# Probabilities times values in three f32r products, and the two mixing norms' weights moved into w_out's rows

## The chip, the core and the metric

The kernel runs on one core of one Trainium2 chip. The metric is the device time of one execution in microseconds. The profile's engines are PE (matmul) with its weight loads shown apart as PEld, DVE (vector), ACT (scalar), POOL, and SP, which issues most DMAs. The operand type f32 is full float32. f32r ("fp32r" in the profile) is a float32 that its producer has rounded to fewer mantissa bits; the matmul rows of the profile write f32 for both.

## What is computed

One inference step of a hybrid decoder layer, for a prompt of 1024 tokens and for 8 running sequences of 8 new tokens each. Around the mixing stage stand two SwiGLU layers (width 2816) with norms. The mixing stage is what the change touches:

```python
  h = pre_mix(x); z = h @ w_in + b_in
    group A: sliding-window GQA (window 128) with learned sinks, banded blocks of 128 queries
    group B: HGRN2 gated linear recurrence, 4 heads of 128
  x = x + post_mix(concat(norm(attn_out), gate(hgrn_out)) @ w_out)

p = sink_probs(s, mask, sink)                       # softmax with a sink in the denominator
out = einsum('bnhgqk,bnkhd->bnqhgd', p, vv)         # probabilities times values
a = rms_norm(a, attn_out_norm[l])                   # over all 512 attention channels
o = rms_norm(o, hg_out_norm[l]) * silu(hg)          # over 128 channels of each head
mix = concatenate([a, o], axis=-1) @ w_out[l]
```

Each attention head has width 64; 8 query heads share 2 key/value heads (g = 0, 1). A query block of 128 sees two key blocks, its own and the one before it (the very first only its own).

## The kernel before

**Tokens.** They go in three groups: n = 0 (256 prompt tokens and the 64 sample tokens, 320 wide), n = 1 and n = 2 (384 prompt tokens each). The engines' order is made by a scheduler that places the instructions by its own simulated times; buffers come from pools with a fixed number of slots, and an instruction that fills a slot waits until the slot's last reader is done.

**Large products.** Every large matrix product is split into three (`mm3`, lines 295 to 299): each operand is a rounded part ("hi", f32r, a cast on ACT, line 274) and a remainder ("lo", DVE, line 275), and PE adds hi by hi (L297), hi by lo (L298) and lo by hi (L299). Weights are loaded by SP into `raw` (3 slots), split by `load_w` into two tiles of the pool `wsp` (8 slots, so four hi/lo pairs), and used.

**Mixing.** `w_in_units(n)` makes z; `w_out_units(n)` (lines 1466 to 1493) multiplies the normed outputs by w_out. For n = 0 it loads w_out in 8 tiles of 128 output columns, each [128, 8, 128]; for n = 1 and 2 in 8 tiles each of [128, 2, 512]. Between them, spread over the large products by `tick()`, run the generators of the attention blocks (`attn_block`, 8 of them) and of the recurrence blocks (`hgrn_block`, 8), and two more for the sample tokens.

**One attention block** goes in two halves (`pr`). Each half makes four score tiles (L1129), the masked maxima (L1137), the exponentials (L1146), then for g = 0 and 1 transposes the probabilities into one PSUM bank (L1155) and copies the bank to a tile `t` of the pool `t2` (L1158: by DVE for g = 0, by ACT for g = 1). After a `yield` the values product follows (L1168): for each head and key block one f32 matmul with the transposed probabilities [128 keys, 128 queries] as weights and the values `vn` [128 keys, 64 channels] as the moving operand. In the program these are 120 matmuls; the profile shows 240 records, two for each f32 matmul.

**Around it.** `finish_attn` scales the block's rows by the root of the mean square and by `aon`, the attention norm's weights broadcast to all partitions (L1103). The gate `z["g"]` is multiplied by the column of `hg_out_norm` (L1089). `vn` is copied out of PSUM by ACT (L1056), one tile for a group. `kv_out` and `sample_attn` store rows of `vn`. The recurrence's tiles come from the pool `m2` (6 slots), `t2` has 8 slots; `t2` also serves the norms and `xt`, the residual rows that SP loads (L441).

## Time and profile before

| what | value |
|---|---|
| median of 3 runs | 1993.19 us (1992.47 to 1993.76) |
| the profiled execution, its own time | 1995.67 us |
| its span in the profile | 1994.0 us |
| granted PE clock, mean | 0.997 |
| busy: PE, DVE, ACT, POOL | 1978.9, 1360.6, 945.8, 591.2 us |
| values product L1168 on PE | 240 records, 29.3 us |

How to read it: a row of a group gives line, engine, operation, the tile written and the tiles read, the sizes, the count, then busy time, mean length of one in ns, idle time before it and what ended that. PE records overlap, since matmuls are pipelined, so what one costs is read in the timeline from one start to the next. In the timeline a row is start, length, engine, line, operation, tiles, size, count; equal neighbours are merged. A row by windows gives for each stretch the busy time of the five engines with their counts, the clock, the DMA share and the rate.

### The profile page before, as it was taken

The numbers are of one execution on the slowest core, as the hardware profiler recorded it, in microseconds if no ns is written. First come the engines' busy times: TensorE is split into PE (matmuls) and PEld (weight loads), VectorE is DVE, ScalarE is ACT, GpSimd is POOL, SyncE is SP. The second block draws the span as 40 slices with busy tenths as digits, with TensorE's granted clock in tenths as the row PEclk, the third lists the DMA queues.
The fourth block names the chain that finished last, engine by engine and source line by source line (L and its number), as shares of the span: only waits on it lengthen the run. The fifth ranks groups of instructions, "written<-read, shape, count | busy, mean of one in ns | idle before, by whom it ended". The sixth has DMA issues, their size and how long they took to land.

```text
span 1994.0 us, 34474 instructions
## 1 busy us (share of the span) xinstructions
PE 1978.9 (99%) x13345; PEld 1856.2 (93%) x13345; DVE 1360.6 (68%) x1979; ACT 945.8 (47%) x1677; POOL 591.2 (30%) x559
## 2 busy tenths in 40 slices
PE   9999999999999999999999999999999999999998
PEld 8999999999998988798899898999999999999887
DVE  5676657886557666875566665755888888655666
ACT  7534333444455445643444555655544444444453
POOL 0013333555104002311123423301165565510202
PEclk9999999999999999999999999999999999999999
DMA  8444435555767645665444343556565555577874
GB/s 260 144 154 160 154 130 188 179 201 204 240 217 227 184 130 175 221 194 146 135 109 147 96 123 93 175 153 205 157 198 203 192 191 189 209 232 234 287 261 141
DMA packets 373694, 360.86 MB, mean 181 GB/s; under 512 B 41662, under 2 KB 295433, under 8 KB 373513
## 3 DMA queue, kind: packets, MB, share of 16 engines
q1 hardware_dynamic: 372729, 357.21, 56.9%
q8 instruction: 105, 1.72, 0.4%
q10 hardware_dynamic: 800, 1.44, 0.2%
q14 instruction: 60, 0.49, 0.1%
HBM read 280.64 MB, written 78.94 MB: 180 GB/s over the span
## 4 chain that ended last, share of the span: by engine, by line
PE 94%; DMA 2%; DVE 2%; issue 1%; ACT 0%; POOL 0%; SPq 0%; DVEq 0%; POOLq 0%; ACTq 0%
PE mm L297 28%; PE mm L299 28%; PE mm L298 28%; PE c L299 1%; PE c L297 1%; PE c L298 1%; PE pv L1168 1%; DMA raw<-in_ffn_w_gu_dram 1%; PE sc L1129 1%; PE lv L1204 1%; PE pT L1155 1%; DMA ar<-fa 1%; PE tr L518 1%; PE l L1228 0%; PE av L1283 0%
## 5 line engine op out<-in xcount | busy, mean ns | idle before, releaser
L297 PE MATMUL mm<-h,wsph 128*128 128x320 f32 (+1 forms) x1296 | 415.2, 322 | 0.0
L298 PE MATMUL mm<-h,wsph 128*128 128x320 f32 (+1 forms) x1296 | 411.0, 318 | 0.1
L299 PE MATMUL mm<-h,wspl 128*128 128x320 f32 (+1 forms) x1296 | 410.5, 317 | 0.1
L274 ACT CAST wsph<-raw 128x1024 fp32r<-128x1024 f32 x202 | 211.2, 1047 | 303.3 <-PE mm L298 235.0
L275 DVE TENSOR_TENSOR wspl<-raw,wsph 128x1024 fp32r<-128x1024 f32 x202 | 251.7, 1248 | 150.9 <-ACT wsph L274 145.6
L275 DVE TENSOR_TENSOR w<-raw,w 128x512 fp32r<-128x512 f32 (+1 forms) x226 | 245.4, 1089 | 93.9 <-ACT w L274 91.9
L274 ACT CAST w<-raw 128x512 fp32r<-128x512 f32 (+1 forms) x226 | 169.5, 754 | 213.4 <-PE mm L298 116.4
L297 PEld LDWEIGHTS mm<-h,wsph 128*128 128x128 f32 x1296 | 243.9, 189 | 5.2 <-issue 3.0
L298 PEld LDWEIGHTS mm<-h,wsph 128*128 128x128 f32 x1296 | 244.4, 189 | 2.6 <-issue 1.4
L299 PEld LDWEIGHTS mm<-h,wspl 128*128 128x128 f32 x1296 | 244.3, 189 | 1.7 <-issue 0.9
L297 PE MATMUL mm<-h,w 128*128 128x384 f32 x704 | 235.6, 335 | 0.6 <-DVE big L745 0.6
L298 PE MATMUL mm<-h,w 128*128 128x384 f32 x704 | 235.6, 335 | 0.0
L299 PE MATMUL mm<-h,w 128*128 128x384 f32 x704 | 230.3, 335 | 0.0
L297 PE MATMUL mm<-w,h 128*128 128x512 f32 x462 | 181.6, 396 | 2.3 <-DVE big L925 1.5
L729 POOL TENSOR_TENSOR big<-big 128x384 f32<-128x384 f32 x88 | 111.5, 1267 | 238.9 <-ACT big L742 127.8
L298 PE MATMUL mm<-w,h 128*128 128x512 f32 x462 | 180.5, 391 | 0.0
L299 PE MATMUL mm<-w,h 128*128 128x512 f32 x462 | 179.7, 393 | 0.0
L275 DVE TENSOR_TENSOR w<-t,w 128x512 fp32r<-128x512 f32 x176 | 158.7, 911 | 14.8 <-ACT w L274 14.6
L268 POOL TENSOR_TENSOR sm<-sm,mhalf 128x3 f32<-128x3 f32 (+4 forms) x38 | 35.7, 939 | 395.0 <-DVE sm L351 169.8
L297 PEld LDWEIGHTS mm<-h,w 128*128 128x128 f32 x704 | 132.1, 188 | 1.0 <-DVE big L745 0.9
L298 PEld LDWEIGHTS mm<-h,w 128*128 128x128 f32 x704 | 132.1, 188 | 0.0
L299 PEld LDWEIGHTS mm<-h,w 128*128 128x128 f32 x704 | 131.7, 188 | 0.1
(351 smaller groups left out, 4038.0 us busy)
## 6 DMA issues: line engine op xcount, KB each, us to landing
raw<-in_ffn_w_gu_dram SPq DMA_DIRECT2D x156, 512.0 KB
raw<-in_ffn_w_down_dram SPq DMA_DIRECT2D x74, 512.0 KB
raw<-in_w_in_dram SPq DMA_DIRECT2D x54, 512.0 KB
ar<-fa SPq DMA_DIRECT2D x70, 384.0 KB
big<-in_ffn_w_down_dram SPq DMA_DIRECT2D x88, 256.0 KB
fb<-big SPq DMA_DIRECT2D x44, 512.0 KB
raw<-fb SPq DMA_DIRECT2D x40, 512.0 KB
fa<-big SPq DMA_DIRECT2D x22, 768.0 KB
```

The source lines that it names most:

```text
L268: G.tensor_tensor(y, x, mhalf[:y.shape[0], :y.shape[1]], op=ALU.pow)
L274: S.copy(hi, src)
L275: (lo_eng or V).tensor_tensor(lo, src, hi.bitcast(F32), op=ALU.subtract)
L297: PE.matmul(out, a[0], b[0], start=first, stop=False, skip_group_check=resume)
L298: PE.matmul(out, a[0], b[1], start=False, stop=False, skip_group_check=resume)
L299: PE.matmul(out, a[1], b[0], start=False, stop=last, skip_group_check=resume)
L518: PE.transpose(bank[:, i * P:(i + 1) * P], y[kh][:, i, k * P:(k + 1) * P], ident)
L729: G.tensor_tensor(e[:, i], e[:, i], e[:, i + 1], op=ALU.mult)
L1129: PE.matmul(banks[g][:, i * 256:i * 256 + wk], zq[64 * g:64 * g + 64, 2 * pr + i, b * P:(b + 1) * P], kx[64 * g:64 * g + 64, k0:k0 + wk], ...
L1155: PE.transpose(bank[:, (i * nk + kb) * P:(i * nk + kb + 1) * P], pt[g][:, i, kb * P:(kb + 1) * P], ident)
L1168: PE.matmul(ob[:, c:c + 64], pT[g][:, (i * nk + kb) * P:(i * nk + kb + 1) * P], vn[:, vb, g * 64:g * 64 + 64], start=kb == 0, stop=kb == n ...
L1204: PE.matmul(b4[cs, a, :32], x[:, a, cs], y[:, a, cs], start=True, stop=True)
```

## The change

1. **Values product.** The transposed probabilities are split like a weight: an ACT cast and a DVE remainder for g = 0 and for g = 1, each in a tile of `t2` (four tiles a half where there were two). `vn` becomes two f32r tiles, hi and lo. The product is `mm3`, so 360 f32r matmuls of [128, 128] by [128, 64] stand where 120 f32 ones stood.
2. **Norm weights.** `attn_out_norm` and `hg_out_norm` come as eight columns in `cols`, one for each 128 rows of w_out, and `load_w` has an argument `gain`: each 128-row piece of w_out is scaled while it is split, by an ACT activation with a scale and a DVE scalar_tensor_tensor for each piece. `aon` with its two DMAs and the gate's multiplication L1089 go; L1103 becomes a tensor_scalar with the root alone.
3. **Room.** `m2` has 5 slots instead of 6, and the transposed keys `kn` go back into `K`. `vn` has 4 slots of the same size instead of 2. Where whole values are stored, `whole` adds hi and lo on DVE into a new `t2` tile first.

```diff
-    def load_w(src, pool, tag, bufs, shape=(P, KC, P)):
+    def load_w(src, pool, tag, bufs, shape=(P, KC, P), gain=None):
...
-        split(hi, lo, raw)
+        if gain is None:
+            split(hi, lo, raw)
+        for k in range(shape[1] if gain is not None else 0):
+            g = gain[:, k:k + 1]
+            S.activation(hi[:, k], raw[:, k], AF.Copy, scale=g)
+            V.scalar_tensor_tensor(lo[:, k], raw[:, k], g, hi[:, k].bitcast(F32), op0=ALU.mult, op1=ALU.subtract)
...
-            return tp.tile(list(shape), F32, tag="m2", bufs=6, name=uid("m2"))
-
-        aon = tp.tile([P, 512], F32, tag="aon", name="aon")
...
+            return tp.tile(list(shape), F32, tag="m2", bufs=5, name=uid("m2"))
...
-            vn = VN[n] = tp.tile([P, 4, P], F32, tag="vn", bufs=2, name=uid("vn"))
+            vn = VN[n] = [tp.tile([P, 4, P], F32R, tag="vn", bufs=4, name=uid("vn")) for _ in range(2)]
...
-                G.tensor_copy(vn[:, 0], VN[n - 1][:, NPB[n - 1]])
+                for new, old in zip(vn, VN[n - 1]):
+                    G.tensor_copy(new[:, 0], old[:, NPB[n - 1]].bitcast(F32))
...
-                S.copy(vn[:r, 1 + i], bank[:r, i * P:(i + 1) * P])
+                split(vn[0][:r, 1 + i], vn[1][:r, 1 + i], bank[:r, i * P:(i + 1) * P])
...
-            V.tensor_scalar(z["g"][:, :, :w], z["g"][:, :, :w], cols[:, C_HGN:C_HGN + 1], None, op0=ALU.mult)
...
-            V.scalar_tensor_tensor(o[:r], o[:r], sm[:r, 1, 0:1], aon[:r], op0=ALU.mult, op1=ALU.mult)
+            V.tensor_scalar(o[:r], o[:r], sm[:r, 1, 0:1], None, op0=ALU.mult)
...
-                    t = t2()
-                    (S.copy if g else V.tensor_copy)(t[:, :2 * wk], bank[:, :2 * wk])
-                    pT.append(t)
+                    hi, lo = [tmp2("pT", dt=F32R) for _ in range(2)]
+                    split(hi[:, :2 * wk], lo[:, :2 * wk], bank[:, :2 * wk])
+                    pT.append((hi, lo))
...
-                            PE.matmul(ob[:, c:c + 64], pT[g][:, (i * nk + kb) * P:(i * nk + kb + 1) * P],
-                                      vn[:, vb, g * 64:g * 64 + 64], start=kb == 0, stop=kb == nk - 1)
+                            cs = slice((i * nk + kb) * P, (i * nk + kb + 1) * P)
+                            mm3(ob[:, c:c + 64], [t[:, cs] for t in pT[g]],
+                                [t[:, vb, g * 64:g * 64 + 64] for t in vn], kb == 0, kb == nk - 1)
...
-            kn = m2((P, 4, P))
+            kn = K
...
+        def whole(vn, r):
+            t = tmp2("vs", (P, P))
+            V.tensor_tensor(t[:r], vn[0][:r, 3].bitcast(F32), vn[1][:r, 3].bitcast(F32), op=ALU.add)
+            return t[:r]
...
-                    wt = load_w(w_out_rows(0, 4, d * P, d * P + P) + w_out_rows(4, 8, d * P, d * P + P), pp, "wsp", 8)
+                    wt = load_w(w_out_rows(0, 4, d * P, d * P + P) + w_out_rows(4, 8, d * P, d * P + P), pp, "wsp", 8,
+                                gain=cols[:, C_AON:C_AON + 8])
...
-                    wt = load_w(w_out_rows(2 * kk, 2 * kk + 2, hf * 512, hf * 512 + 512), pp, "wsp", 8, (P, 2, 512))
+                    wt = load_w(w_out_rows(2 * kk, 2 * kk + 2, hf * 512, hf * 512 + 512), pp, "wsp", 8, (P, 2, 512),
+                                cols[:, C_AON + 2 * kk:C_AON + 2 * kk + 2])
```

The change adds 9 lines ahead of most of the places above, so the old L297 to L299 are L306 to L308 now, and the old L275 is L279.

**PE, the first half of the first attention block** (`mm` is a z tile of `w_in`, `pv` the values product's bank, `t` the transposed probabilities). Before:

```order
L299 MATMUL mm_6831<-h_6072,wspl_6828 128x320
L1168 MATMUL pv_6857<-vn_6386,t_932_6786 128x64
L1168 MATMUL pv_6857<-vn_6386,t_934_6791 128x64
L1168 MATMUL pv_6857<-vn_6386,t_932_6786 128x64
L1168 MATMUL pv_6857<-vn_6386,t_934_6791 128x64
L297 MATMUL mm_6868<-h_6071,wsph_6864 128x320
```

The same place now (the first two product groups of four; `vn_6385` and `pT_6789` are rounded parts, `vn_6386` and `pT_6790` remainders):

```order
L308 MATMUL mm_6838<-h_6074,wspl_6835 128x320
L306 MATMUL pv_6864<-vn_6385,pT_6789 128x64
L307 MATMUL pv_6864<-vn_6386,pT_6789 128x64
L308 MATMUL pv_6864<-vn_6385,pT_6790 128x64
L306 MATMUL pv_6864<-vn_6385,pT_6796 128x64
L307 MATMUL pv_6864<-vn_6386,pT_6796 128x64
L308 MATMUL pv_6864<-vn_6385,pT_6797 128x64
```

Four rows have become twelve, at the same place between the same two large products.

**DVE, while w_out's tiles for n = 0 are split** (`wspl` is a remainder, `cm`, `m` and `lv` belong to the recurrence, `big` in L1089 is the gate). Before:

```order
L275 TENSOR_TENSOR wspl_9959<-raw_9954,wsph_9958 128x1024
L1089 TENSOR_SCALAR big_9525<-big_9525,cols 128x1536
L1223 COPY_PREDICATED cm_9654<-lm_90,lv_9803 128x128
L1239 TENSOR_TENSOR m_1410_9647<-m_1410_9647,m_1412_9649 128x128x2
L275 TENSOR_TENSOR wspl_10017<-raw_10012,wsph_10016 128x1024
L1158 COPY t_1439_9849<-pT_9844 128x512
```

Now:

```order
L293 SCALAR_TENSOR_TENSOR wspl_10092<-raw_10087,cols,wsph_10091 128x128 x8
L1227 COPY_PREDICATED cm_9726<-lm_90,lv_9888 128x128
L1243 TENSOR_TENSOR m_1419_9719<-m_1419_9719,m_1421_9721 128x128x2
L293 SCALAR_TENSOR_TENSOR wspl_10164<-raw_10159,cols,wsph_10163 128x128 x8
L279 TENSOR_TENSOR pT_9949<-pT_9943,pT_9948 128x512
L279 TENSOR_TENSOR pT_9958<-pT_9952,pT_9957 128x512
```

Each remainder is eight instructions, the gate's row is gone, and one copy of a probabilities bank has become two remainders.

**SP, the end of the ffn1 pairs that run beside the first attention blocks** (`raw<-fb` are ffn weights for PE, `xt` residual rows in `t2` slots, `x1N` rows stored). Before:

```order
L900 DMA raw_8169<-fb_117 128x2x512
L441 DMA xt_7995<-in_x_prompt_dram 128x512
L441 DMA xt_7999<-in_x_prompt_dram 128x512
L441 DMA xt_8035<-in_x_prompt_dram 128x512
L441 DMA xt_8039<-in_x_prompt_dram 128x512
L441 DMA xt_8043<-in_x_prompt_dram 128x512
L441 DMA xt_8047<-in_x_prompt_dram 128x512
L444 DMA x1N_98<-big_5726 128x512
L900 DMA raw_8221<-fb_117 128x2x512
```

Now:

```order
L909 DMA raw_8286<-fb_117 128x2x512
L450 DMA xt_8044<-in_x_prompt_dram 128x512
L450 DMA xt_8048<-in_x_prompt_dram 128x512
L450 DMA xt_8100<-in_x_prompt_dram 128x512
L450 DMA xt_8104<-in_x_prompt_dram 128x512
L453 DMA x1N_98<-big_5728 128x512
L450 DMA xt_8108<-in_x_prompt_dram 128x512
L453 DMA x1N_98<-big_6008 128x512
L450 DMA xt_8112<-in_x_prompt_dram 128x512
L453 DMA x1N_98<-big_5728 128x512
L909 DMA raw_8358<-fb_117 128x2x512
```

The last two `xt` loads stand behind stores of the rows that the first ones served, and the next weight load (`raw_8221` before, counted from the loads around it `raw_8286` now) stands ahead of all six.

More of the change, by code (lines that the diff above doesn't have):

```diff
@@ L192, in gains @@
         put(C_LB, A["hg_lb_logits"].rearrange("l (c p) -> (l c) p", p=P), 8)
-        put(C_HGN, A["hg_out_norm"], 1)
+        for half in range(2):
+            nc.sync.dma_start(
+                rows[C_AON:C_AON + 4, half * 64:half * 64 + 64],
+                A["attn_out_norm"][0:1, half * 256:half * 256 + 256].rearrange("o (m d) -> (o m) d", d=64))
+        nc.sync.dma_start(rows[C_AON + 4:C_AON + 8, :], A["hg_out_norm"].partition_broadcast(4))
         bank = axbank()
@@ L321, in new_h, with tmp2 @@
         return [[hslot(n), hslot(n)], [hslot(n), hslot(n)]]
-    def tmp2(name, shape=(P, 512)):
-        return pp.tile(list(shape), F32, tag="t2", bufs=8, name=uid(name))
+    def tmp2(name, shape=(P, 512), dt=F32):
+        return pp.tile(list(shape), dt, tag="t2", bufs=8, name=uid(name))
     def bcast_steps(part, w, out):
@@ L1308, in sample_attn @@
             vsc = dr.tile([NS, P], F32, name="vsc")
-            nc.sync.dma_start(vsc, vn[:NS, 3])
+            nc.sync.dma_start(vsc, whole(vn, NS))
             vnew = tmp2("vnew", (P, 512))
@@ L1386, in sample_hgrn @@
                 PE.transpose(tb[:r, a], K[:, a, :r], ident)
-            kn = m2((P, 4, P))
+            kn = K
             V.tensor_copy(kn[:r], tb[:r])
@@ L1426, in kv_out @@
             if n == 0:
-                for i, src in ((5, kn[:r, :P]), (6, vn[:r, 3])):
+                for i, src in ((5, kn[:r, :P]), (6, whole(vn, r))):
                     for b in range(8):
```

10 lines of the change are left out of this document (3 added, 7 removed).

## Prediction

> **What bounds the kernel now.** I read the page's busy times first, then the chain that ended last, then PE's waits.
>
> ```profile
> span 1994.0 us, 34474 instructions
> PE 1978.9 (99%) x13345; PEld 1856.2 (93%) x13345; DVE 1360.6 (68%) x1979; ACT 945.8 (47%) x1677; POOL 591.2 (30%) x559
> PE 94%; DMA 2%; DVE 2%; issue 1%; ACT 0%; POOL 0%; SPq 0%; DVEq 0%; POOLq 0%; ACTq 0%
> ```
>
> PE is busy for 99% of the span and is 94% of the chain, so nearly all that is added to PE's own queue is added to the time, and what is added elsewhere costs only where it makes PE wait. The view of PE's waits has nine rows; the first and the last:
>
> ```profile
> PE mm L297 <- DVE big L925: 1.5, 1, 1.5
> ...
> PE ax L173 <- DMA rows<-in_norm_ffn_pre_dram: 0.2, 1, 0.2
> ```
>
> They sum to 7.3 us, and no wait is over 1.5 us. Faster helpers can win back a part of these 7.3 us and no more. The profiled execution took 1995.67 us, 1.67 more than its span, and 2.48 more than the median of 1993.19; I work out changes on the span and add them to the median.
>
> **The price of one small matmul.** The change turns 120 f32 matmuls into 360 f32r ones. I read what one costs in PE's timeline, from start to start, at a block that stands between large products:
>
> ```profile
> 1096.35 0.33 PE L298 MATMUL mm<-h,wsph 128*128 128x384 f32 x1
> 1096.53 0.33 PE L299 MATMUL mm<-h,wspl 128*128 128x384 f32 x1
> 1096.70 1.89 PE L1168 MATMUL pv<-vn,t 128*128 128x64 f32 x16
> 1098.40 0.48 PE L297 MATMUL mm<-wsph,h 128*128 128x512 f32 x1
> 1098.72 0.40 PE L298 MATMUL mm<-wspl,h 128*128 128x512 f32 x1
> 1098.95 0.40 PE L299 MATMUL mm<-wsph,h 128*128 128x512 f32 x1
> ```
>
> A large f32r product of 384 columns starts 0.17 to 0.18 us after the one before, one of 512 columns 0.23. The sixteen records run from 1096.70 to 1098.40, and the first product behind them lasts 0.32 us to the next start instead of 0.23, which is theirs as well: 1.70 + 0.09 = 1.79 us, 112 ns a record. The group has 240 records:
>
> ```profile
> L1168 PE MATMUL pv<-vn,t 128*128 128x64 f32 x240 | 29.3, 272 | 0.0
> L1168 PEld LDWEIGHTS pv<-vn,t 128*128 128x128 f32 x240 | 28.9, 191 | 0.3
> ```
>
> That is 240 x 0.112 = 26.9 us on PE now. What are the 112 ns made of? Other short f32 matmuls with 128-column weights tell:
>
> ```profile
> 1084.99 0.71 PE L348 MATMUL st<-omean,ss 128*128 128x1 f32 x6
> 1085.63 0.44 PE L297 MATMUL mm<-h,wsph 128*128 128x384 f32 x1
> ...
> 1157.83 0.94 PE L1290 MATMUL u<-big,m 128*128 128x128 f32 x7
> 1158.62 1.90 PE L1168 MATMUL pv<-vn,t 128*128 128x64 f32 x16
> ```
>
> With 128 moving columns a record costs 0.79 / 7 = 113 ns, with one column 0.64 / 6 = 107 ns at least, though two of these six load only 64 columns. So the price does not depend on the moving columns: it is that of getting 128 columns of weights in. The same load stands before every f32r matmul:
>
> ```profile
> L297 PEld LDWEIGHTS mm<-h,wsph 128*128 128x128 f32 x1296 | 243.9, 189 | 5.2 <-issue 3.0 <-ACT wsph L274 0.3
> 707.11 0.19 PEld L299 LDWEIGHTS mm<-wsph,h 128*128 128x128 f32 x1
> 707.33 0.13 PEld L297 LDWEIGHTS mm<-wsph,h 128*64 128x64 f32 x1
> ```
>
> An f32r load of 128 columns is recorded with 189 ns against 191 for the f32 one, and half the columns take 0.06 us less, so it too pays by the column. In the large products it hides, because 320 to 512 moving columns last longer; with 64 columns nothing hides it. I therefore price an f32r product of 64 columns at 112 ns: 360 x 0.112 = 40.3 us, **13.4 us more than now, all on PE**. The bounds: from above, the one-column row with its whole tail (0.64 us and the 0.11 by which the next start comes late, over six) gives 124 ns, so 44.6 us, +17.7. From below, the bare 1.70 / 16 = 106 ns for the new ones gives 38.2, +11.3. Far below lies the bare streaming of 64 columns: (0.230 - 0.175) / 128 = 0.43 ns a column from the 512- and 384-column paces above, so 0.175 - 320 x 0.00043 = 37 ns; that is a rival, not my value, because no short matmul above comes near it.
>
> **DVE and ACT, the probabilities.** In each of 16 halves one DVE copy and one ACT copy become two casts and two remainders. The nearest rows are the copies and the split of the block's output, which also reads PSUM:
>
> ```profile
> L1158 DVE COPY t<-pT 128x512 f32<-128x512 f32 x14 | 9.5, 682 | 1.9 <-PE pT L1155 1.7
> L1158 ACT COPY t<-pT 128x512 f32<-128x512 f32 x14 | 8.2, 588 | 13.4 <-PE pT L1155 13.4
> L1095 DVE TENSOR_TENSOR h<-oT,h 128x512 fp32r<-128x512 f32 x8 | 5.4, 680 | 0.0
> ```
>
> DVE gets 16 x 0.68 = 10.9 us more, ACT 16 x 0.59 = 9.4 us, and the way from transposes to values product grows from one copy, 0.68 us, to two casts and a remainder, 2 x 0.59 + 0.68 = 1.86 us: 1.2 us longer. The cover is the time between copy and product:
>
> ```profile
> 1133.77 0.68 DVE L1158 COPY t<-pT 128x512 f32<-128x512 f32 x1
> 1133.86 0.59 ACT L1158 COPY t<-pT 128x512 f32<-128x512 f32 x1 [4.98 <-PE pT L1155]
> ...
> 1137.42 1.89 PE L1168 MATMUL pv<-vn,t 128*128 128x64 f32 x16
> ...
> 1310.35 0.59 ACT L1158 COPY t<-pT 128x512 f32<-128x512 f32 x1 [2.48 <-PE pT L1155]
> ...
> 1312.51 0.33 PE L1168 MATMUL pv<-vn,t 128*128 128x64 f32 x2
> ```
>
> 3.0 us there, but 1.6 near the end of the mixing stage, where the products of the last blocks follow their copies at once. A remainder now waits on DVE for its cast, and behind it in DVE's queue stand splits of weights and steps of the recurrence, for which PE waits later; the wait is one cast, 0.59 us, at most. I price it all at nothing where large products fill the time; without cover each of the last three halves loses up to 1.2 us.
>
> **w_out's scaling.** For n = 0 each of 8 tiles is split by 8 + 8 instructions of 128 columns instead of 1 + 1 of 1024; for n = 1, 2 each of 16 tiles by 2 + 2 of 512. Nearest rows:
>
> ```profile
> L275 DVE TENSOR_TENSOR wspl<-raw,wsph 128x1024 fp32r<-128x1024 f32 x202 | 251.7, 1248 | 150.9 <-ACT wsph L274 145.6 <-PE mm L299 4.8
> L1295 DVE SCALAR_TENSOR_TENSOR st<-st,m,u 128x128 f32<-128x128 f32 x28 | 7.8, 342 | 3.0 <-PE u L1290 3.0
> L443 DVE SCALAR_TENSOR_TENSOR big<-big,sm,xt 128x512 f32<-128x512 f32 x30 | 22.0, 769 | 9.2 <-DMA xt<-in_x_prompt_dram 5.9 <-DMA xt<-x1N 2.0 <-POOL sm L268 1.0
> L274 ACT CAST wsph<-raw 128x1024 fp32r<-128x1024 f32 x202 | 211.2, 1047 | 303.3 <-PE mm L298 235.0
> L1252 ACT ACTIVATE m<-av 128x128 f32<-128x128 f32 x32 | 8.4, 275 | 1.9 <-PE av L1286 1.8
> ```
>
> DVE, n = 0: 64 x 7.8 / 28 = 17.8 us for 8 x 1.25 = 10.0, +7.8; the others 32 x 22.0 / 30 = 23.5 for 20.0, +3.5. ACT, n = 0: at most 64 x 0.275 = 17.6 for 8.4, +9.2. The cover for n = 0 is long, since these tiles are split far ahead:
>
> ```profile
> 965.63 1.22 DVE L275 TENSOR_TENSOR wspl<-raw,wsph 128x1024 fp32r<-128x1024 f32 x1
> L1476 ACT COPY big<-mm x8: 402/420/426, 984.5 to 1017.9; 128x320 f32<-128x320 f32 x8
> 985.00:1020.00 35.00, 35.00 (x349) 33.35 (x348) 19.90 (x36) 17.50 (x41) 6.46 (x11) 1.00 0.47 116
> ```
>
> The first split starts at 965.63, its product is evicted at 984.5, and in the 35 us of the stage DVE is busy for 19.9 and ACT for 17.5, which leaves 15 and 17 for 8 and 9. Nothing reaches PE. If that cover were gone, the price would be the excess, 1.0 us a tile.
>
> **What is removed** is on DVE alone: the gate's multiplication, and the broadcast product at 0.84 us, for which a tensor_scalar of 0.52 stands.
>
> ```profile
> L1089 DVE TENSOR_SCALAR big<-big,cols 128x1536 f32<-128x1536 f32 x2 | 2.1, 1064 | 3.1 <-ACT big L1088 3.1
> L1103 DVE SCALAR_TENSOR_TENSOR t<-t,sm,aon 128x512 f32<-128x512 f32 x8 | 6.7, 842 | 2.1 <-POOL sm L268 2.0
> L496 DVE TENSOR_SCALAR big<-big,sm 128x512 f32<-128x512 f32 x12 | 5.6, 524 | 2.5 <-POOL sm L268 2.5
> ```
>
> PE waits for neither (no such row among its nine), so it wins nothing; DVE saves some 6 us against the 22 above. The few splits of `vn`, the two `whole` sums, the DMAs of the norms, one slot less in `m2` and the copy of the keys into `K` go together at nothing: each is under 0.7 us, once or a few times, off PE.
>
> **Buffers and queues.** Four `t2` slots of eight are now held from the splits of a half to its product, where two were. In SP's queue two `xt` loads and the weight load behind them now stand behind stores, in a stretch in which DVE is already nearly full:
>
> ```profile
> 800.00:850.00 50.00, 48.35 (x388) 39.41 (x389) 43.45 (x71) 31.23 (x66) 16.94 (x17) 1.00 0.69 219
> ```
>
> DVE 43.45 of 50 us, and PE idle for 1.65: the place of the mixing stage where helpers are late now. One half's extra remainder (0.68 us) and the later loads fall here. I charge 1.0 us of new PE waits; from -1.5 us (the wait on L925 goes, since the order shifts) to +4 (this stretch and the last three halves at 1.2 us each).
>
> **Sum.** 1993.19 + 13.4 + 1.0 = **2007.6 us**. Lower end: 1993.19 + 11.3 - 1.5 = 2003.0. Upper end: 1993.19 + 17.7 + 4 = 2014.9. A measurement of this kernel can tell about 0.2%, 4.0 us, from no change.
>
> **Rivals.** (1) *The loads do not bind in f32r, and the time falls.* If f32r weights came in fast enough, a product would cost its 37 ns of streaming: 360 x 0.037 = 13.3 us, 13.6 less than now: 1979.6. It decides from 26.9 / 360 = 75 ns downward. For it: no f32r matmul of the trace is short, so its load is never seen alone. Against it: 189 ns beside 191. The Trainium skill has two rules on this side. "TensorE: Matmul & The Clock Gate", section on weight-path perf modes, has a fast weight load for 128-column weights whose type is not FP32; whether f32r counts as FP32 is not said there, and the equal lengths of the loads speak against it here. "FP8 and Floating Point Precision", section TensorE Precision Notes, counts four passes for true FP32 and names a reduced FP32 that is truncated when it is read; if that takes one pass, three f32r products are three quarters of one f32 product, an estimate of 26.9 x 0.75 = 20.2 us and 1986.5 us in all, but the trace's price does not go by what is streamed. Chance 8%: 6% faster, 2% within 0.2%.
>
> (2) *Helpers become the bound.* If DVE, 87% full between 800 and 850, or the four held `t2` slots make PE wait over 4 us, say 1 us in 8 of the 16 halves, the time is 1993.19 + 13.4 + 8 = 2014.6, and beyond 2014.9 with the upper price. For it: the row of that stretch; against it: 3.0 us of cover in most halves. Chance 12%.
>
> (3) *f32r with 64 columns is carried out like f32, in two records each.* 720 x 0.112 = 80.6 us, +53.7: 2046.9. For it: nothing; against it: in the timeline rows above L298, L299 and L297 follow each other with one record each, while the f32 product has two. Chance 2%.
>
> **How the numbers follow.** The forecast has the other 78%. Range 2003 to 2015; the forecast, and the half of (2) that is under its end, make 84% of it, less what the two prices leave out. Faster by over 0.2%: 6%. Within: 2%. Slower: 78 + 12 + 2 = 92%.
>
> **What would show it.** Right: 360 records of the new product, sixteen old ones' 1.79 us become 24 at about 2.7 us; PE's busy time up by about 13 us, its waits still under 12 us in sum; DVE's busy time up by 15 to 20 us with no effect. Wrong: a pace under 75 ns, 720 records, or waits of PE on the remainders of `pT` in several halves.

## The result and the profile after

| what | before | after |
|---|---|---|
| median | 1993.47 us (4 runs, 1992.47 to 1993.81) | 2015.57 us (4 runs, 2013.36 to 2019.57) |
| ratio | | 1.0109, 95% interval 1.0093 to 1.0126 |
| span of the profiled execution | 1994.0 us | 2011.8 us (its time 2013.50) |

The kernel became slower, as forecast, but by 22.1 us instead of 14.4, and 0.6 us over the end of the range. The first lines of the page after, engines and counts:

```profile
span 2011.8 us, 34902 instructions
PE 1996.7 (99%) x13465; PEld 1872.7 (93%) x13465; DVE 1380.5 (69%) x2076; ACT 970.0 (48%) x1765; POOL 589.3 (29%) x561
```

PE is busy 17.8 us longer and the span is 17.8 us longer. DVE has 19.9 us more, as forecast, and ACT 24.2, where the terms of the prediction make 18.6. The new product, in the groups and in PE's timeline at the block whose sixteen records the prediction priced:

```profile
L306 PE MATMUL pv<-vn,pT 128*128 128x64 f32 x120 | 32.3, 269 | 0.0
L307 PE MATMUL pv<-vn,pT 128*128 128x64 f32 x120 | 33.2, 277 | 0.0
L308 PE MATMUL pv<-vn,pT 128*128 128x64 f32 x120 | 33.0, 275 | 0.0
L306 PEld LDWEIGHTS pv<-vn,pT 128*128 128x128 f32 x120 | 23.0, 191 | 0.3
```

```profile
1104.33 0.33 PE L308 MATMUL mm<-h,wspl 128*128 128x384 f32 x1
1104.50 0.19 PE L306 MATMUL pv<-vn,pT 128*128 128x64 f32 x1
1104.53 0.27 PE L307 MATMUL pv<-vn,pT 128*128 128x64 f32 x1
1104.64 0.28 PE L308 MATMUL pv<-vn,pT 128*128 128x64 f32 x1
...
1106.98 0.28 PE L308 MATMUL pv<-vn,pT 128*128 128x64 f32 x1
1107.09 0.47 PE L306 MATMUL mm<-wsph,h 128*128 128x512 f32 x1
1107.41 0.39 PE L307 MATMUL mm<-wspl,h 128*128 128x512 f32 x1
```

360 records, one start every 0.11 us, 24 in 2.59 us; the load is 191 ns as before. Summed from each record's start to the next instruction's, the values product takes 39.9 us where it took 26.2: +13.7. That leaves 4.1 us of the span, and 8.4 of the medians. PE's waits show almost none of it; the first and last of nine rows, 7.7 us in sum (7.3 before). Over the whole span PE is idle for 15.1 us, as before:

```profile
PE l L1232 <- DVE m L1243: 2.2, 1, 2.2
...
PE ax L173 <- DMA rows<-in_norm_ffn_pre_dram: 0.2, 1, 0.2
```

Most of the rest stands in a column that the prediction did not read, the granted clock. The view by windows of the changed kernel (busy time of PE, PEld, DVE, ACT, POOL, then PEclk, DMA share, GB/s), in stretches of 3.4 us:

```profile
813.40:816.90 3.50, 3.50 (x60) 3.33 (x58) 2.33 (x4) 2.49 (x5) 0.00 (x0) 1.00 0.89 311
816.90:820.30 3.40, 3.40 (x12) 2.72 (x9) 3.40 (x6) 1.53 (x5) 1.20 (x1) 0.50 0.87 305
820.30:823.70 3.40, 3.40 (x16) 2.77 (x16) 1.74 (x7) 2.70 (x7) 1.10 (x2) 1.00 0.90 292
834.00:837.40 3.40, 1.24 (x20) 0.76 (x20) 3.40 (x6) 2.00 (x4) 3.32 (x5) 1.00 0.88 282
837.40:840.80 3.40, 3.40 (x13) 3.11 (x14) 3.40 (x6) 2.54 (x6) 1.31 (x3) 0.50 0.06 15
1308.40:1311.80 3.40, 3.40 (x42) 3.17 (x41) 3.00 (x4) 2.06 (x4) 1.94 (x1) 1.00 0.39 113
1311.80:1315.20 3.40, 3.40 (x18) 2.95 (x17) 0.99 (x1) 0.00 (x0) 0.00 (x0) 0.50 0.31 90
```

Three single windows of 3.41 us are granted half the clock. One comes right behind a stretch in which PE mostly waited (834 to 837); the other two come behind stretches that hold 24 values products and 32 or 16 small products of the recurrence, and in which PE was busy all the time. In PE's timeline the first of them begins right behind these:

```profile
816.26 0.28 PE L308 MATMUL pv<-vn,pT 128*128 128x64 f32 x1
816.46 0.46 PE L1208 MATMUL lv<-m,m 128*32 128x32 f32 x32
816.85 0.79 PE L307 MATMUL mm<-w,h 128*128 128x512 f32 x1
817.44 0.63 PE L308 MATMUL mm<-w,h 128*128 128x512 f32 x1
817.87 0.63 PE L306 MATMUL mm<-w,h 128*128 128x512 f32 x1
...
820.00 0.54 PE L308 MATMUL mm<-w,h 128*128 128x512 f32 x1
820.38 0.40 PE L306 MATMUL mm<-w,h 128*128 128x512 f32 x1
820.62 0.39 PE L307 MATMUL mm<-w,h 128*128 128x512 f32 x1
```

Products of 512 columns start every 0.43 us instead of 0.23, with no idle time that any wait could name. A window so loses 3.41 x (1 - 0.23 / 0.427) = 1.57 us and lowers the mean clock by 3.41 x 0.5 / 2014 = 0.00085. The profile of before has one such window beside those of the start and the end, at 916 us; after has three.

### The profile page after: what moved, and what is told of

It is laid out like the page before. It is cut to its first block, busy times and chain, and to the rows that moved or that the text cites. A ratio compares the mean times of both kernels' runs of the same rounds, so it can differ in the third digit from the quotient of the medians.

```text
span 2011.8 us, 34902 instructions
## 1 busy us (share of the span) xinstructions
PE 1996.7 (99%) x13465; PEld 1872.7 (93%) x13465; DVE 1380.5 (69%) x2076; ACT 970.0 (48%) x1765; POOL 589.3 (29%) x561
## 4 chain that ended last, share of the span: by engine, by line
PE 94%; DMA 3%; DVE 2%; issue 1%; ACT 0%; POOL 0%; SPq 0%; DVEq 0%; POOLq 0%; ACTq 0%
PE mm L306 27%; PE mm L307 27%; PE mm L308 27%; PE c L306 1%; PE c L308 1%; PE c L307 1%; DMA raw<-in_ffn_w_gu_dram 1%; PE sc L1132 1%; PE lv L1208 1%; PE pT L1158 1%; PE pv L307 1%; PE pv L308 1%; PE pv L306 1%; DMA xt<-in_x_prompt_dram 1%; PE tr L527 1%
## 5 line engine op out<-in xcount | busy, mean ns | idle before, releaser
L306 PE MATMUL mm<-h,wsph 128*128 128x320 f32 (+1 forms) x1296 | 415.1, 322 | 0.0
L308 PE MATMUL mm<-h,wspl 128*128 128x320 f32 (+1 forms) x1296 | 410.8, 318 | 0.0
L279 DVE TENSOR_TENSOR w<-raw,w 128x512 fp32r<-128x512 f32 (+1 forms) x226 | 245.5, 1090 | 97.4 <-ACT w L278 95.6
L278 ACT CAST wsph<-raw 128x1024 fp32r<-128x1024 f32 x178 | 186.2, 1047 | 254.9 <-PE mm L307 192.2
L279 DVE TENSOR_TENSOR wspl<-raw,wsph 128x1024 fp32r<-128x1024 f32 x178 | 221.3, 1245 | 119.8 <-ACT wsph L278 119.0
L306 PEld LDWEIGHTS mm<-h,wsph 128*128 128x128 f32 x1296 | 243.9, 189 | 5.3 <-issue 3.4
L308 PEld LDWEIGHTS mm<-h,wspl 128*128 128x128 f32 x1296 | 243.9, 188 | 1.0 <-issue 0.5
L306 PE MATMUL mm<-h,w 128*128 128x384 f32 x704 | 235.8, 335 | 0.6 <-DVE big L754 0.6
L308 PE MATMUL mm<-h,w 128*128 128x384 f32 x704 | 230.5, 335 | 0.0
L306 PE MATMUL mm<-w,h 128*128 128x512 f32 x462 | 182.8, 398 | 0.6 <-ACT h L278 0.4
L308 PE MATMUL mm<-w,h 128*128 128x512 f32 x462 | 180.4, 394 | 0.0
L279 DVE TENSOR_TENSOR w<-t,w 128x512 fp32r<-128x512 f32 x176 | 161.3, 926 | 18.0 <-ACT w L278 17.7
L306 PEld LDWEIGHTS mm<-h,w 128*128 128x128 f32 x704 | 132.2, 188 | 1.0 <-DVE big L754 0.9
L308 PEld LDWEIGHTS mm<-h,w 128*128 128x128 f32 x704 | 131.7, 188 | 0.1
```

The lines of the kernel that those rows point to most:

```text
L278: S.copy(hi, src)
L279: (lo_eng or V).tensor_tensor(lo, src, hi.bitcast(F32), op=ALU.subtract)
L306: PE.matmul(out, a[0], b[0], start=first, stop=False, skip_group_check=resume)
L308: PE.matmul(out, a[1], b[0], start=False, stop=last, skip_group_check=resume)
```

## The theories

**T1**, the prediction's: a small product costs its weight load, 112 ns, and the rest lies beside PE's work. **T2**: the long runs of f32r products with 64 columns also leave PE's multiplying array too little to do, and the clock is halved for the window that follows, more or less often by where a run falls in the windows. **T3**: the helpers' added work, the four held `t2` slots or SP's order make PE wait, above all between 800 and 850 us. Three measures tell them apart in each profile: the sum of the values product; PE's idle time between 800 and 850 us (1.65 us before); the single halved windows.

## The experiments

**The changed kernel again.**

> The changed kernel, unaltered, timed again beside the kernel before. The first theory (the 120 more small products cost 112 ns each on PE and nothing else costs anything) expects +13.7 us, 2007. The second (the long runs of small f32r products also make the granted clock halve for single windows of 3.4 us, each of which loses about 1.6 us, more or fewer by where the runs fall in the windows) expects +17 to +22, with a spread of 4 to 6 us among the executions, a mean granted clock that is lower the longer the execution, and 2 to 5 such windows in the profile besides the one at the start. The third (the helpers' added work makes PE wait) expects +17 to +22 with PE's waits some 4 us longer in sum than the 7.3 us of before.

2015.90 us (2014.34 to 2016.89) beside 1992.58 of before; ratio 1.0106, 1.009 to 1.0122. The windows view, first of this run, then of the first profile of after:

```profile
800.00:850.00 50.00, 44.13 (x379) 35.52 (x379) 39.00 (x67) 28.74 (x63) 14.90 (x17) 0.97 0.63 201
1148.00:1151.90 3.90, 3.90 (x56) 3.61 (x56) 0.10 (x1) 0.00 (x0) 0.00 (x0) 1.00 0.49 138
1151.90:1155.50 3.60, 3.60 (x15) 3.60 (x15) 2.77 (x4) 2.54 (x3) 1.93 (x5) 0.54 0.00 0
```

```profile
800.00:850.00 50.00, 47.20 (x388) 38.37 (x389) 41.53 (x70) 30.10 (x64) 14.92 (x17) 0.93 0.67 211
```

PE idles 5.9 us between 800 and 850 us (2.8 in the first profile), and three windows are halved, at 838, 1152 and 1210 us. The same kernel loses in both ways, and in different proportions. T1 alone is refuted: it expected 2007 us.

**w_out split as before, the norm weights left out.** `load_w` is called without `gain`.

> The changed kernel with w_out split as before, in one ACT and one DVE instruction a tile; the two norms' weights are left out of the computation altogether, so nothing else takes over their work. Against the changed kernel of the same call: the first and second theories expect no difference beyond the spread (within 3 us), since the scaling lies beside PE's work; the third expects 2 to 5 us less, with PE's waits shorter by as much.

2018.30 us (2014.97 to 2020.51), ratio 1.0118 (1.0102 to 1.0134): no gain. The profile has three halved windows and 4.9 us idle between 800 and 850. Taking the scaling out of the changed kernel wins nothing.

**Two products of three.**

```diff
-                            mm3(ob[:, c:c + 64], [t[:, cs] for t in pT[g]],
-                                [t[:, vb, g * 64:g * 64 + 64] for t in vn], kb == 0, kb == nk - 1)
+                            v = vn[0][:, vb, g * 64:g * 64 + 64]
+                            PE.matmul(ob[:, c:c + 64], pT[g][0][:, cs], v, start=kb == 0, stop=False)
+                            PE.matmul(ob[:, c:c + 64], pT[g][1][:, cs], v, start=False, stop=kb == nk - 1)
```

> The changed kernel with two of the three products (rounded by rounded, remainder of the probabilities by rounded values; rounded probabilities by remainder of the values is left out), 240 f32r records where before has 240 f32 ones. All helpers work as in the changed kernel. The first theory expects the time of before, within 1 us. The second expects 0 to 4 us over before: runs of 16 records take 1.8 us and fill half of a window of 3.4 us, so the clock halves once or twice more than before at most. The third expects 4 us over before or more, as PE's waits, since the helpers have all of the change's work.

2005.73 us (2005.38 to 2007.65), ratio 1.006 (1.0047 to 1.0073): 13.1 over before with as many loads as before. The values product takes 26.8 us (26.2 before), so the price of 112 ns holds; PE is idle for 7.4 us at 800 to 850, 5.7 more than before:

```profile
PE l L1233 <- POOL m L1246: 4.2, 1, 4.2
PE lv L1209 <- DVE m L1244: 2.0, 1, 2.0
PE mm L306 <- DVE big L934: 1.6, 1, 1.6
```

T3 is needed; T1's expectation missed by 12 us.

**Half as many f32 products again, everything else as before.**

```diff
+                        if nk == 2 or i == 0:
+                            PE.matmul(ob[:, c:c + 64], pT[g][:, i * nk * P:i * nk * P + P],
+                                      vn[:, b + (1 if first else 0), g * 64:g * 64 + 64], start=True, stop=True)
                         for kb in range(nk):
```

> The kernel before, in whose values product the first key block's f32 product stands twice (the first result is overwritten), so 360 f32 records stand where 240 did: as many weight loads as in the changed kernel, with all helpers as before. All theories expect +13.4 us from the loads. The second adds: an f32 product goes through the array in two records, so the array is busier in these runs than with f32r, and the clock halves less often than in the changed kernel: +13 to +16, spread under 3 us. If it halves as often, +17 to +20, the activity of the array is not what decides.

2006.41 us (2006.11 to 2008.49), ratio 1.0063 (1.005 to 1.0076): +13.8. The product takes 39.6 us, no window is halved, and PE idles 1.3 us at 800 to 850:

```profile
800.00:850.00 50.00, 48.69 (x414) 39.55 (x400) 43.81 (x70) 30.63 (x65) 17.41 (x17) 1.00 0.69 217
```

So 120 more loads alone cost 13.4 of product and 13.8 of time, as T1 priced them. The changed kernel's other 8.3 to 9.5 us (of 22.1 and 23.3) are not the loads.

**The kernel before with four held slots.** Each bank is copied in two halves into two tiles.

```diff
-                    t = t2()
-                    (S.copy if g else V.tensor_copy)(t[:, :2 * wk], bank[:, :2 * wk])
+                    t = [t2(), t2()]
+                    for i in range(2):
+                        (S.copy if g else V.tensor_copy)(t[i][:, :wk], bank[:, i * wk:i * wk + wk])
```

> The kernel before with its f32 values product, but each bank of transposed probabilities is copied in two halves into two tiles of t2, so that four slots are held from the copies to the product as in the changed kernel; nothing else is altered. If the held slots are what delays the stretch of 800 to 860 us (the last two xt loads then stand behind stores in SP's queue, DVE's L443 and the recurrence's steps come later, PE waits): 4 to 7 us over before, with a wait of PE of over 2 us near 834 us. If the added work of DVE and ACT delays it, or the clock alone: within 2 us of before (16 more copies on DVE and 16 on ACT are small).

1998.99 us (1995.25 to 2001.15, 11 runs), ratio 1.0023 (1.0015 to 1.0032), +5.8. The profiled run is the fastest of the eleven and still has the wait, of 2.8 us:

```profile
PE l L1229 <- DVE h L476: 2.8, 1, 2.8
```

SP's rows in the timeline show how: the last two `xt` loads stand behind stores again, so DVE's sums of these rows, and the steps behind them, come later.

```profile
805.97 1.88 SPq L441 DMA_DIRECT2D xt<-in_x_prompt_dram  x4
...
810.85 0.33 SPq L444 DMA_DIRECT2D x1N<-big  x1
811.27 0.38 SPq L441 DMA_DIRECT2D xt<-in_x_prompt_dram  x1
811.75 0.39 SPq L444 DMA_DIRECT2D x1N<-big  x1
812.18 0.45 SPq L441 DMA_DIRECT2D xt<-in_x_prompt_dram  x1
```

So the slots cost time without any f32r. This profile shows 4.0 us of idle PE at 800 to 850, 2.3 more than before; the rest of the median's +5.8 is not seen in it.

**Two products, remainders in slots of their own.** `lo` comes from a pool of two slots in the room of the values' remainder.

> The kernel with two of three products, whose remainders of the probabilities lie in two slots of a pool of their own, in the room that the remainder of the values took (the remainder of the values is left out, of the stored values too); t2 has two slots held as before, and all casts and remainders of the probabilities and w_out's scaling stay. If the held slots are the cause of the loss at 811 to 860 us: 5 to 8 us less than with the remainders in t2 (2005.7), so 1998 to 2001, with SP's xt loads ahead of the stores again and no wait over 2 us near 834. If the helpers' work is the cause: no change, 2004 to 2007.

1998.10 us (1996.57 to 2000.19), ratio 1.0025 (1.0016 to 1.0033): 7.6 less than with the remainders in `t2`. SP's `xt` loads stand ahead of the stores, and the wait near 830 us is short:

```profile
PE l L1233 <- DVE m L1244: 1.4, 1, 1.4
```

With the one before: the slots are shown from both sides. Neither edit moves slots alone, though: the one before has twice as many copies of half the size, and this one leaves out the values' remainder and its subtractions, 9 short instructions on DVE.

**Two heads at a time** (transposes, splits and products for i = 0, then for i = 1, with a `yield` between).

> The changed kernel with the probabilities transposed, split and multiplied for two heads (one of each key/value head) at a time: two slots of t2 are held at once instead of four, and a run of the product has 12 records (1.3 us) instead of 24 (2.7 us); one step more in each half. Complete computation. If held slots and long runs are the two causes beside the loads' +13.7: 2007 to 2010, 5 to 8 us less than the changed kernel, with at most one halved window. If the helpers' work is the cause: no less than 2014.

2014.81 us (2014.21 to 2015.29), ratio 1.0104 (1.0091 to 1.0118). No window outside the start is halved and PE idles 2.7 us at 800 to 850, and yet nothing is won. Start to start, scores, transposes and large products take 2.1, 2.2 and 2.7 us more than before; why was not followed up. The time is the one expected if the helpers' work is the cause. But the run doesn't free T3's queue either: in SP's order four of the six `xt` loads (814.3 to 815.7 us) stand behind the first two stores (810.7 and 811.3 us). So it decides between slots and helpers in neither direction, and about 7 us of it stay unexplained; that no window is halved with runs of 12 fits T2.

**Pieces of six.** A `yield` after each head of the product.

> The changed kernel with a step of the generator after each head of the values product, so that its 24 records fall into four pieces of 6 (0.7 us) with other products of PE between them; the four slots of t2 are held longer than in the changed kernel. Complete computation. The theory of the clock: no halved window from the values product, 3 to 5 us less from that; the theory of the slots: 811 to 860 us is as slow as in the changed kernel or slower. Together 2011 to 2016; under 2010 if only the clock counts, over 2016 if only the slots.

2022.39 us (2018.92 to 2023.94), ratio 1.0137 (1.012 to 1.0153): the worst of all, and T2's expectation missed. But the pieces did not stay apart: the scheduler put several of them side by side, and PE's order still has runs of 16, 17 and 18 records (833.1, 1194.5, 1162.5 us). One halved window, at 1165 us, comes behind the run of 18, with PE busy; the two other halved stretches follow waits of PE:

```profile
829.00:833.70 4.70, 2.46 (x34) 2.14 (x32) 4.70 (x6) 3.31 (x8) 3.24 (x6) 1.00 0.36 106
833.70:840.50 6.80, 6.69 (x27) 5.86 (x27) 6.31 (x10) 2.26 (x5) 0.61 (x1) 0.50 0.81 255
1321.00:1325.20 4.20, 1.41 (x13) 0.80 (x12) 2.81 (x11) 4.15 (x10) 0.61 (x1) 1.00 0.00 1
1325.20:1335.40 10.20, 8.94 (x39) 8.41 (x40) 2.61 (x6) 3.69 (x8) 0.00 (x0) 0.50 0.24 69
```

A wait is paid twice when a halved window follows it. What runs of six would do is not shown; the waits that this edit brings cost more than it could win.

**360 loads, own slots** (the kernel of two products with the second one doubled).

> The kernel of two products with slots of their own for the remainders of the probabilities, in which the product of these remainders stands twice: 360 f32r records again, as many loads as in the changed kernel, two slots of t2 held as before. The result counts that product twice and leaves out the remainder of the values. If the loads (+13.4 on that kernel's 1998.1), the held slots and the clock are all there is: 2011.5 and 0 to 3 for halved windows, so 2011 to 2014, 2 to 5 us less than the changed kernel. If the held slots cost nothing once 360 products fill PE: 2015 to 2017.

2014.44 us (2011.78 to 2016.14), ratio 1.0106 (1.0092 to 1.012): not separable from the changed kernel. PE idles 1.9 us at 800 to 850 and one window is halved, but that is its fastest run. This kernel differs from the one of two products with own slots by 120 more f32r records alone. It takes 16.3 us longer, where 120 more f32 records took 13.8. The values product accounts for 13.5 of the 16.3. The mean clock falls from 0.9967 (11 runs) to 0.9953 (4 runs), which at 0.00085 and 1.57 us a window is about 1.7 windows or 2.7 us (an estimate), with the slots and the helpers' work the same on both sides. That is about the rest, though another execution of this kernel, below, has a wait as well.

**128 moving columns.** The moving operand is `t[:, vb]`, both key/value heads.

> The changed kernel, in which each of the 360 products moves 128 columns of values (both key/value heads) instead of 64: the same loads, the same helpers, twice the streaming; what the second 64 columns give is overwritten or wrong. If the 112 ns are the load's, PE's time stays within 1 us. The theory of the clock (the array is too idle in the long runs of 64-column products): the halved windows go, but perhaps the one behind the wait at 834 us; 2 to 4 us less than the changed kernel, 2011 to 2014. If the array's activity is not what decides: 2015 to 2017, with as many windows as before.

2013.36 us (2012.54 to 2014.23), ratio 1.0102 (1.0088 to 1.0116). The product takes 40.6 us, 0.7 more for twice the streaming, so the load binds. One window is halved, behind a wait of 4.2 us; none follows a run. That is T2's expectation, though the intervals of the times overlap.

**Operands exchanged.**

```diff
-                            mm3(ob[:, c:c + 64], [t[:, cs] for t in pT[g]],
-                                [t[:, vb, g * 64:g * 64 + 64] for t in vn], kb == 0, kb == nk - 1)
...
+                        mm3(ob[:, 256 * pr:256 * pr + 256], [t[:, vb] for t in vn],
+                            [t[:, :2 * wk].rearrange("p (i k q) -> p k i q", i=2, k=nk)[:, kb] for t in pT[g]],
+                            kb == 0, kb == nk - 1)
```

> The changed kernel with the operands of the three products exchanged: the values of one key block (128 columns, both heads) are the weights and the probabilities of two query heads (256 columns) are moving, so 180 f32r products instead of 360. The result is laid out the other way round and is wrong; all that follows runs as it is. If a product costs its load or its streaming, whichever is longer, at 256 columns 0.12 us (from 0.175 at 384 and 0.23 at 512 columns): 180 x 0.12 = 21.8 for 39.9 us, 18 less, and fewer halved windows: 1995 to 1999. If every record costs more than that: over 2003.

1998.52 us (1996.17 to 2000.83), ratio 1.0028 (1.0018 to 1.0038). Two rows of its timeline:

```profile
1026.62 0.28 PE L308 MATMUL pv<-pT,vn 128*128 128x256 f32 x1
1026.74 0.28 PE L306 MATMUL pv<-pT,vn 128*128 128x256 f32 x1
```

0.12 us a product at 256 columns, four times the streaming for the price of one load; 23.1 us for the product. The result lies the other way round; what it would cost to turn it back is not in this time. PE's wait at 833 us (4.2 us) and the halved windows behind it are still there.

**w_out's scaling alone.**

> The kernel before with w_out's rows scaled while they are split and the two norms' multiplications gone, the f32 values product, its slots and its copies as before. If the scaling lies beside PE's work: 1992 to 1995, as before. If its smaller instructions on ACT and DVE delay PE: 2 to 5 us over before.

1996.66 us (1992.49 to 2001.28), ratio 1.0016 (1.0007 to 1.0025): +3.4, in the range that was expected if the smaller instructions delay PE. The profile (of an execution of 1995.51) does not show such a delay. Where w_out is used PE is full, DVE has 23.5 us where it had 19.9 and ACT 24.4 where it had 17.5.

```profile
985.00:1020.00 35.00, 35.00 (x349) 33.35 (x348) 23.50 (x65) 24.44 (x72) 5.43 (x10) 1.00 0.48 118
```

**Four more profiles.** Two more of that kernel, one of before, one of the 360 loads with own slots:

> The kernel of w_out's scaling alone, for a second profile; its executions went from 1992.5 to 2001.3 us, and the one that was profiled (1995.5) loses nothing in the mixing stage against before. If what the slower ones lose is the stretch of 811 to 860 us (DVE's late steps and PE's wait on the recurrence) or single halved windows, a profile of over 1996 us shows over 2 us in PE's wait near 833 us or a halved window outside the start; if the scaling itself delays PE, PE waits between 985 and 1030 us.

> The same kernel of w_out's scaling alone once more, a third profile, with the same reading: the losses of an execution over 1996 us lie at 811 to 860 us and in halved windows, or else between 985 and 1030 us where w_out's tiles are used.

> The kernel before, unaltered, for a second profile: executions from 1991.3 to 2000.4 us were timed. Single halved windows outside the start, none to three of them at 1.6 us each, and PE's wait of 1 to 2 us near 834 us are expected to make up the difference between this execution and the 1995.7 us one.

> The kernel with 360 records and slots of its own for the remainders, for a second profile: its executions went from 2011.8 to 2016.1, and the one profiled was the fastest, with one halved window outside the start. If the clock makes the difference, an execution of 2014 or more shows two to four halved windows behind runs of 24 records, and no wait over 2 us near 834 us; if the stretch at 811 to 860 us makes it, a wait of over 2 us there.

The two of w_out's scaling took 1994.47 and 1992.73 us, neither over 1996; no window outside start and end is halved and no wait is new. What its slower runs lose stays open; the mean clock of its eleven runs, 0.9965 against 0.9973, would be one halved window more, 1.6 us (an estimate). Before took 1996.08, with one halved window at 917 us. The 360 loads with own slots took 2015.73: three halved windows (839, 1150, 1208 us), and a wait after all, on the cast of a tile that SP loaded late (`ar`, issued between 831 and 835 us):

```profile
PE mm L306 <- ACT h L278: 3.9, 1, 3.9
```

SP's waits between 800 and 850 us in that run name something the prediction had priced at nothing: the round trip of the sample tokens' values through DRAM. `whole` makes a new tile first, so the store moved from row 298 of SP's order to row 359, right ahead of the loads that read it back.

```profile
SPq L1320 <- DMA vsc<-vs: 5.4, 1, 5.4
```

**The store moved back, alone and with own slots.**

```diff
+            if n == 0:
+                vsc = VN["vsc"] = dr.tile([NS, P], F32, name="vsc")
+                nc.sync.dma_start(vsc, whole(vn, NS))
...
-            vsc = dr.tile([NS, P], F32, name="vsc")
-            nc.sync.dma_start(vsc, whole(vn, NS))
+            vsc = VN["vsc"]
```

> The changed kernel with one thing moved: the sum of the sample tokens' two value tiles, and its store to DRAM, stand right behind the split of the values, where the store stands in the kernel before (row 299 of SP's order against 298; in the changed kernel row 359, right ahead of the loads that read it back, for which SP stands still for 4 to 5.4 us with ffn weights, ar and cache loads behind it). Complete computation. If SP's standing is a cause of the loss at 811 to 860 us: 2 to 5 us less than the changed kernel (2015.6 to 2015.9), 2011 to 2014. If only the four held slots and the clock are: no change, 2014.5 to 2017.

> The kernel with 360 records and slots of its own for the remainders, and the early store as well: both causes of late loads at 811 to 860 us are gone, the loads of 120 more products and the halved clock windows of their runs are left (the remainder's product counts twice, the values' remainder is left out). If these are the causes: 1993.3 + 13.4 and 1 to 3 us for windows, so 2007 to 2010, 4 to 7 less than without the early store (2014.4), and no wait of PE over 2 us near 834 us. If the stretch is slow for another reason, the helpers' work: 2012 to 2016.

Alone: 2017.97 us (2016.19 to 2021.19), ratio 1.0131 (1.0114 to 1.0148), no gain; SP's wait on the store is gone, PE's at 835 us (3.3) is not, and PE idles 7.6 us at 800 to 850, more than in the changed kernel. So the store alone is not the cause. With own slots: 2012.66 us (2010.88 to 2015.88), ratio 1.0102 (1.0087 to 1.0117), over the 2007 to 2010 expected and inside the 2012 to 2016 expected if the helpers' work slows the stretch. The profile, of the shortest execution (2010.88), has the stretch clean and two halved windows, at 1144 and 1202 us:

```profile
800.00:850.00 50.00, 48.40 (x414) 39.60 (x414) 43.65 (x74) 31.61 (x66) 16.87 (x17) 1.00 0.71 220
1140.00:1220.00 80.00, 80.00 (x754) 73.14 (x753) 45.74 (x102) 42.16 (x91) 18.93 (x30) 0.96 0.35 102
```

No kernel of the study is faster than before.

## Why the prediction was right in direction and too low

Three terms nearly account for the spans of these seven profiles (us against before's 1994.0, with PE's idle time between 800 and 850 us less before's 1.65, and windows at 1.57 each, less before's one):

| profile | values product | idle 800 to 850 | windows | sum | span |
|---|---|---|---|---|---|
| after | +13.7 | +1.2 | 3: +3.1 | +18.0 | +17.8 |
| after, again | +13.6 | +4.2 | 3: +3.1 | +21.0 | +21.2 |
| early store | +13.9 | +5.9 | 2: +1.6 | +21.4 | +21.3 |
| 360, own slots, again | +13.5 | +2.7 | 3: +3.1 | +19.3 | +20.0 |
| store and slots | +13.5 | 0.0 | 2: +1.6 | +15.1 | +15.2 |
| 128 moving | +14.4 | +3.1 | 1: 0 | +17.5 | +16.8 |
| f32, 360 records | +13.4 | -0.3 | 0: -1.6 | +11.5 | +10.6 |

In others more is missing: two products sum to 7.9 and measure 11.9, 360 loads with own slots 13.7 and 16.1; there PE idles between 1270 and 1330 us too, 1.4 and 0.7 us. Pieces of six sum to 23 and measure 28.2, two heads at a time to 12 and 19.4. The middle term is that of one stretch: with PE's idle time of the whole span in its place, the seven sums fall 0.4 to 2.2 us short of the spans. So the table shows where most of the time went, not all of it.

1. **The price of a small product** was right: +13.7 for 13.4 predicted, by the two products (240 f32r loads take 26.8 us where 240 f32 ones took 26.2), by 120 more f32 records (+13.4) and by 128 moving columns (+0.7). Rival 1 falls with 0.11 us a start, rival 3 with 360 records.
2. **Probabilities on DVE and ACT**: the busy times came nearly as priced (DVE +10.4 us for 10.9, ACT +8.4 for 9.4). No wait of PE on `pT` is in the first profile of after.
3. **w_out's scaling**: no profile shows a wait of PE on it, and leaving it out of the changed kernel won nothing. ACT has 41.4 us of it where the plain splits took 25.0; the prediction priced 9.2 more, for n = 0, and nothing for n = 1 and 2. Alone it is 3.4 us slower in the median, which no profile places, so "Nothing reaches PE" is not confirmed. What is removed from DVE comes to 4.6 us by the prediction's own rows (2.1 and 8 x 0.32), not 6; the sum does not depend on it.
4. **Buffers and queues** is the first step that failed: "I charge 1.0 us of new PE waits". The place was right, 800 to 850 us, and the size was not: PE's idle time there grew by 1.2 and 4.2 us in two profiles of the same kernel. In one profile of a kernel with nothing else four held slots bring 2.3 us of it (+5.8 in the time), and two products without them are 7.6 us faster. "The two `whole` sums ... go together at nothing" was too quick: the sum costs 0.3 us, but it moved a store 61 rows down SP's queue. Moving it back alone did nothing; with own slots the stretch was clean, in one profile. So 1.0 us fits the first profile of after and not the second, and no run gives it as the size of either cause.
5. **The granted clock** has no term in the sum, which is the second failure. The 26 runs of the five kernels with 360 f32r records of 64 columns in runs of up to 24 (the changed kernel in two sets) have a mean clock of 0.9947, 57 runs of before 0.9973: 0.0026 / 0.00085 makes 3 more halved windows, about 5 us (an estimate). The profiles, most of them of executions under the median, show 1 to 3 such windows where that of before has one: 1.4 more on average, 2.2 us. The six runs with 360 f32 records have 0.9975, so it is not the number of loads; four with 128 moving columns 0.9962.

   That the array's low activity is the cause fits all these, and the traces go further. The clock changes on a grid of 3.41 us in each trace. Counted in PE's timelines, 62 windows of that grid in the seven profiles of these five kernels hold 18 or more of the 64-column records. Of the 35 with four or more large products beside them (`mm`) none is followed by a halved window, of the 27 with at most three 12 are. With f32 records (4 windows) or 128 moving columns (7) none of the latter kind is. And the window of before, at 916 us, comes behind four records of a product that uses 32 of the 128 rows (L1412, 0.53 us each), with PE busy. So what counts is what shares a window with the run, and the grid lies elsewhere in each execution. It stays a fit: 15 of the 27 were not followed by a halved window, and no run sets the activity by itself.

For the medians that makes 13.7 + about 5 + 1 to 4 for the stretch: 20 to 23, against 22.1 and 23.3 measured; with the 2.2 us that the profiles show for the clock it is 17 to 20. How the last microseconds divide between clock and stretch stays open, since each execution divides them anew. Rival 2 named the mechanism (held slots, DVE late) and nearly the time, 2014.6, but as 1 us in each of 8 halves; it is one place, with the clock on top, so its time is near by luck. The sign "waits still under 12 us" came out right and told nothing, since a halved clock shows as busy time.

## What to carry to other kernels

Price short matmuls by their weight loads, and turn the operands so that the many columns move, if the result may lie the other way round or turning it back is cheaper. When a helper tile is added, look in every queue for what it makes wait and what the order now puts behind that, not only at its own length. Add the PEclk column to the sum: where small products fill most of 3.4 us or PE waits for a few microseconds, a halved window may follow.

## What I had not expected of the hardware

The granted clock fell to 0.50 for exactly one window of 3.41 us, and PE was busy for 3.50 of 3.50 us just before it, with 60 matmuls, among them 24 load-bound ones of 64 columns. The windows lie at other times in each execution: 838, 1152, 1210 us in one, 817, 837, 1312 in another of the same kernel. The Trainium skill, page "TensorE: Matmul & The Clock Gate", Part 1, has a free-running window of 3413 ns and half the clock after an idle one; the window's length and its free phase agree with the traces (3.41 us), but by them a window need not be idle to be followed by a halved one. And an f32r product with 256 moving columns starts 0.12 us after the one before, one with 64 or 128 columns 0.11: up to there the moving columns are almost free.
